# In the two FFNs of a decoder trunk: the gelu and the gate product issued behind the next weight pieces, and another order of the weight pieces in the seven-product chains

## The chip, the core and the metric

The kernel runs on one core of a Trainium2 chip. A core has a matrix engine (TensorE, PE in the profile, with its weight loads shown apart as PEld), VectorE (DVE), ScalarE (ACT), GpSimd (POOL) and SyncE (SP). Each engine works through its own list of instructions in the order in which the program issued them, and waits on semaphores for the others. The metric is the device time of one execution in microseconds; three timed executions of the kernel before stand in the table below.

## The reference

A trunk of two layers on 512 tokens of width 1024, float32. Layer 0 mixes tokens with three groups of dilated window attention, layer 1 with a gated linear recurrence. After each comes the gated ConvFFN that this change is about, between two RMS norms:

```python
def conv_ffn(x, w_up, conv_w, conv_b, w_down):
    u = causal_dwconv(x @ w_up, conv_w, conv_b)      # 3 taps along the tokens
    g, v = u[..., :D_FF], u[..., D_FF:]              # D_FF = 3072
    return (jax.nn.gelu(g, approximate=True) * v) @ w_down
```

## The kernel before

**Operands.** Each float32 matrix is split into a high and a low part (`split`, lines 152 to 154): ScalarE copies the raw tile to `hi` with rounding (L153), VectorE subtracts it from the raw tile to give `lo` (L154). Every product is three passes on TensorE, hi by hi, hi by lo and lo by hi. Raw weights come in 1 MB loads from SP (L280) into three raw buffers; their split halves go into 16 pairs of buffers (`HALVES`). A queue `pieces` holds what is to be split next, and `pump` takes pieces from its front as long as `state["live"]`, the buffers in use, allows it. `tick` is called after each step of TensorE and pumps one or two pieces. So what order the instructions of ScalarE and VectorE have is set by the order of the Python calls, nothing else reorders them.

**The up-projection of an FFN** makes 12 groups j of 256 gate features and 256 value features. A full tile is 128 features by 512 tokens, 24 matmuls (`feat`, L340). `begin` (lines 689 to 697) then computes the 3 taps: one ScalarE instruction (L679) and two on VectorE (L683) from PSUM into `u`; for a gate tile it returns the gelu (ScalarE, L695), for a value tile the product with the gate (VectorE, L697). In groups 0 to 2 and 11 `sink` calls the returned function at once, so gelu and product stand ahead of the pieces that the following `tick` splits.

**The seven-product groups.** In groups 3 to 10 the gate half is computed with seven products of quarter size instead of eight (`seven`, `chain`; matmuls at L833), the value half with full tiles, in four `quarters` each. One group is a cycle of 15 slots on TensorE: the products s1, w11, s4, w12, s2 and s3 stand at slots 0, 3, 4, 8, 9 and 14, a22 at slot 20, so in slot 5 of the next cycle; the eight other slots are quarters of value tiles. The names are those of the left operands, made of the four 512x128 blocks of one weight load: w11 and w12 are plain blocks, a22 too; s1 gets a block added by a DMA from POOL (`ahead`, L191); s2 is s1 + w11, added in place by VectorE once s1 is split (`across`, L205); s4 is w12 + s2, added in place by VectorE once w12 and w11 are split (`upper`, L209); s3 is w11 with a block added by a second DMA from POOL, issued in `upper`, once w11 is split. `stream` lists the pieces of a cycle: each has a place, and all are sorted by place. `value(0)` and `value(1)`, called v0 and v1 below, are the two value tiles of the same group, two buffers each, from the next 1 MB load. The splits of a cycle are issued about one cycle ahead of their use on TensorE.

Each chain has two PSUM banks y0 and y1. In the slot after product s4 the *seed* is issued: ScalarE saves y1 (L843) and overwrites y1 with minus y0 (L844). Product w12 adds to y0, and so waits for the seed. In the first cycle of an FFN there is no a22 of a chain before: slot 5 is empty and the seed follows one quarter later.

**The start of the seven-product part.** While the full tiles of groups 1 and 2 run, `token_sums` forms the right operands (B and T, L749 to L770) on VectorE, with splits, as a side job of the same ticks.

Of the kernel before, what the change touches and what calls it, by code (L numbers as in the profile page):

```python
# [38 lines left out]
SEVEN = range(3, 11)  # L39
# [39 lines left out]
def kernel(  # L79
# [45 lines left out]
    def psum(s="ps"):  # L125
        return pp.tile([P, 512], F32, tag="ps", name=nm(s))
# [34 lines left out]
    def parts_of(kind, raw):  # L161

        if kind == "feat":
            return [raw[:, :, m * P : (m + 1) * P] for m in range(2)]
        if kind == "value":
            return [raw[:, 2 * i : 2 * i + 2, :] for i in range(2)]
        if kind == "rows":
            return [raw[:, i : i + 1, :] for i in range(2)]
        return [raw]
# [12 lines left out]
    def blocks(i):  # L182

        raw = raws[i]
        return {
            n: raw[:, 4 * k : 4 * k + 4, m * P : m * P + P]
            for n, m, k in (("w11", 0, 0), ("w12", 0, 1), ("s1", 1, 0), ("a22", 1, 1))
        }

    def add_rows(to, src):  # L190
        nc.gpsimd.dma_start(to, src, accum_op=ALU.add)  # L191

    def ahead(i):
        assert i < state["dma"]
        add_rows(blocks(i)["s1"], plan[i][3][0][0][:, 4:8, P:256])

    def stream(i0, n):

        items = []
        for c in range(n):  # L200
            i = i0 + 2 * c

            def across(i=i):
                x = blocks(i)
                nc.vector.tensor_tensor(x["s1"], x["s1"], x["w11"], op=ALU.add)  # L205

            def upper(i=i):
                x = blocks(i)
                nc.vector.tensor_tensor(x["w12"], x["w12"], x["s1"], op=ALU.add)  # L209
                add_rows(x["w11"], plan[i][3][0][0][:, 0:4, P:256])  # L210

            def value(m, i=i + 1):
                raw = lambda: parts_of("feat", raws[i])[m]
                return (i, m), lambda: [raw()[:, :4], raw()[:, 4:]], None, m == 1

            for at, item in (
                (-6, (None, lambda i=i: ahead(i))), (0, ("s1", "s1")), (0.1, (None, across)), (1, ("w12", "w12")),
                (2, ("w11", "w11")), (2.1, (None, upper)), (4, ("s4", "w12")), (5, ("s2", "s1")), (6, value(0)),
                (8, ("a22", "a22")), (10, ("s3", "w11")), (11, value(1)),
            ):  # L220
                if c or at >= 0:
                    if isinstance(item[0], str):
                        item = ((i, item[0]), lambda i=i, h=item[1]: [blocks(i)[h]], None, item[0] == "s3")
                    items.append((CYCLE * c + at, item))
        return [item for _, item in sorted(items, key=lambda x: x[0])]
# [19 lines left out]
    def pump(limit=2):  # L245

        for _ in range(limit):
            if not pieces:
                refill()
            while pieces and pieces[0][0] is None:  # L250
                pieces.pop(0)[1]()
            if pieces and state["live"] + 2 - (pieces[0][0][1] in HALF) <= HALVES:
                key, cuts, norm, last = pieces.pop(0)
                cuts = cuts()
                his, los = [], []
                for n, raw in enumerate(cuts):
                    hi, lo = (
                        wp.tile([P] + list(raw.shape[1:]), F32R, tag=t, name=nm("w" + t)) for t in ("hi", "lo")
                    )
                    if norm is not None:  # L260
                        split_normed(hi, lo, raw, norm + n * raw.shape[1])
                    else:
                        split(hi, lo, raw)
                    his.append(hi)
                    los.append(lo)
                units[key] = (his, los)
                state["live"] += len(cuts)
                state["used"] += last
                while pieces and pieces[0][0] is None:
                    pieces.pop(0)[1]()  # L270
            while state["dma"] < len(plan) and state["dma"] - state["used"] < RAW_BUFS:
                load()
# [12 lines left out]
    def chunk():  # L285
        i = state["next"]
        state["next"] += 1
        return i

    def take(i, j):  # L290
        while (i, j) not in units:
            before = state["live"]
            pump(1)
            assert before != state["live"], (i, j, state)
        return units[i, j]

    def done(n=2):
        state["live"] -= n

    def side(steps, delay=1):  # L300
        sides.append([delay, steps])

    def tick():
        for s in list(sides):
            s[0] -= 1
            if s[0] <= 0:
                try:
                    s[0] = next(s[1])
                except StopIteration:
                    sides.remove(s)  # L310
        if not state["hold"]:
            pump(1 if state["even"] or state["live"] >= HALVES - 4 else 2)
# [201 lines left out]
    def feat_tiles(n, hT, sink, halves=False):  # L514

        if halves:
            ids = [chunk() for _ in range(n)]
            W = {}
            banks = [psum() for _ in range(2 * n)]
            for hf in range(2):  # L520
                for j in range(2 * n):
                    if not hf:
                        W[j] = take(ids[j // 2], j % 2)
                    feat(W[j], hT, banks[j], hf * 256, hf * 256 + 256)
                    if hf:
                        done()
                        sink(j, banks[j])
                    tick()
            return
        for c in range(n):  # L530
            i = chunk()
            for m in range(2):
                feat_tile(i, m, hT, lambda ps: sink(2 * c + m, ps))

    def feat_tile(i, m, hT, sink):
        ps = psum()
        feat(take(i, m), hT, ps, 0, S)
        done()
        sink(ps)
        tick()  # L540

    def rows_proj(nchunks, act, order, post, pre, eng=nc.gpsimd):

# [130 lines left out]
    def ffn(layer, hT, post, pre):  # L674
        ca, cc = ffn_cols[layer]

        def conv(ps, j):
            u = gen(s="u")
            nc.scalar.activation(  # L679
                u, ps, AF.Identity, scale=cc[:, j : j + 1], bias=cc[:, 48 + j : 49 + j]  # L680
            )
            for d, wc in ((1, ca[:, 48 + j : 49 + j]), (2, ca[:, j : j + 1])):
                nc.vector.scalar_tensor_tensor(  # L683
                    u[:, d:], ps[:, : S - d], wc, u[:, d:], op0=ALU.mult, op1=ALU.add
                )
            return u

        gv = []

        def begin(b, ps, j):  # L690
            m = b % 2
            u = conv(ps, 24 * (b // 2) + 2 * j + m)
            if b < 2:
                gv.append(u)
                return lambda: nc.scalar.activation(u, u, AF.Gelu_apprx_tanh)  # L695
            g = gv[2 * j + m]
            return lambda: nc.vector.tensor_tensor(g, g, u, op=ALU.mult)  # L697

        def sink(b, ps, j):
            begin(b, ps, j)()  # L700

        order = [([0, 1, 2, 3], range(9)), ([0], range(9, 12)), ([1], range(9, 12))]
        order += [([2, 3], [9]), ([2], [10, 11]), ([3], [10, 11])]
        prep, run = rows_proj(12, act_split(gv), order, post, pre)
        T = []
        for j in range(SEVEN[0]):
            if j == 1:
                side(token_sums(hT, T))
            if j < SEVEN[0] - 1:
                feat_tiles(2, hT, lambda b, ps: sink(b, ps, j), j == 0)  # L710
            else:
                feat_tiles(1, hT, lambda b, ps: sink(b, ps, j))
                i = chunk()
                feat_tile(i, 0, hT, lambda ps: sink(2, ps, j))
        i = seven(hT, T, begin, i)
        x_back()
        prep(3)
        for j in range(SEVEN[-1] + 1, 12):
            for b in range(j == SEVEN[-1] + 1, 4):
                if b % 2 == 0:  # L720
                    i = chunk()
                feat_tile(i, b % 2, hT, lambda ps: sink(b, ps, j))
        return run()

    kept = []
# [677 lines left out]
    hT = attention(hT, (norm_mix_post, 0), (norm_ffn_pre, 0))  # L1403
    hT = ffn(0, hT, (norm_ffn_post, 0), (norm_mix_pre, 1))
    hT = lru(hT, (norm_mix_post, 1), (norm_ffn_pre, 1))
# [29 lines left out]
```

## Time and profile before

| | |
|---|---|
| median of 3 timed executions | 1449.54 us (1449.50 to 1449.74) |
| profiled execution: its time | 1450.94 us |
| profiled execution: span from the first to the last instruction | 1449.1 us |
| mean granted TensorE clock | 0.997 |
| first FFN, seven-product part | from 563.05 us of the span on |
| second FFN, seven-product part | from 1113.03 us of the span on |

In a row of a timeline stand the start in us, the length in us, the engine, the line of the kernel, the operation, the output and inputs by name, the shape, and a count if several are merged; square brackets at the end give the idle time of the engine before it and what ended it. In a row of the table by stretches stand the stretch, its length, the busy time of each engine with its instructions, the granted clock (PEclk), the share of the DMA engines and GB/s.

### The profile page before, as it was taken

The numbers are of one execution on the slowest core, as the hardware profiler recorded it, in microseconds if no ns is written. First come the engines' busy times: TensorE is split into PE (matmuls) and PEld (weight loads), VectorE is DVE, ScalarE is ACT, GpSimd is POOL, SyncE is SP. The second block draws the span as 40 slices with busy tenths as digits, with TensorE's granted clock in tenths as the row PEclk, the third lists the DMA queues.
The fourth block names the chain that finished last, engine by engine and source line by source line (L and its number), as shares of the span: only waits on it lengthen the run. The fifth ranks groups of instructions, "written<-read, shape, count | busy, mean of one in ns | idle before, by whom it ended". The sixth has DMA issues, their size and how long they took to land.

```text
span 1449.1 us, 20565 instructions
## 1 busy us (share of the span) xinstructions
PE 1435.5 (99%) x7437; PEld 1232.3 (85%) x7437; DVE 970.6 (67%) x2115; ACT 735.1 (51%) x1644; POOL 178.3 (12%) x311
## 2 busy tenths in 40 slices
PE   9999999999999999999999999999999999999998
PEld 7888888888888898989988888888898899988886
DVE  6767747464646878877774348769778877764333
ACT  7656636262615555555543335589454655554231
POOL 0341514040402101101000001000100111000000
PEclk9999999999999999999999999999999999999999
DMA  7653536363736254554452322432434545453201
GB/s 225 208 143 114 169 118 198 115 208 106 212 100 210 90 180 89 141 132 105 140 203 87 116 74 88 131 116 73 132 126 125 137 107 140 124 190 116 87 1 59
DMA packets 142847, 189.66 MB, mean 131 GB/s; under 512 B 9313, under 2 KB 119353, under 8 KB 142233
## 3 DMA queue, kind: packets, MB, share of 16 engines
q1 hardware_dynamic: 114280, 145.48, 31.4%
q0 software_dynamic: 27616, 41.82, 12.1%
q8 instruction: 58, 0.95, 0.3%
q10 hardware_dynamic: 848, 1.05, 0.2%
q14 instruction: 45, 0.36, 0.1%
HBM read 168.83 MB, written 19.49 MB: 130 GB/s over the span
## 4 chain that ended last, share of the span: by engine, by line
PE 91%; ACT 4%; DVE 3%; issue 1%; DVEq 0%; ACTq 0%
PE ps L340 43%; PE acc L340 24%; PE ps L833 11%; PE v L1029 8%; PE v L959 1%; DVE xb L1238 1%; DVE wlo L154 1%; PE O L1180 1%; PE S L1125 1%; ACT whi L153 1%; PE S L1079 1%; ACT sig L1259 1%; PE O L340 1%; PE tr L422 1%; ACT sig L1278 0%
## 5 line engine op out<-in xcount | busy, mean ns | idle before, releaser
L340 PE MATMUL ps<-hT,whi 128*128 128x512 f32 (+1 forms) x2240 | 645.0, 373 | 0.0
L340 PEld LDWEIGHTS ps<-hT,whi 128*128 128x128 f32 x2240 | 403.9, 189 | 68.5
L340 PE MATMUL ps<-hT,wlo 128*128 128x512 f32 (+1 forms) x1120 | 415.7, 371 | 0.0
L154 DVE TENSOR_TENSOR wlo<-raw,whi 128x512 fp32r<-128x512 f32 x408 | 269.1, 688 | 186.3 <-ACT whi L153 186.3
L153 ACT ACTIVATE whi<-raw 128x512 fp32r<-128x512 f32 x408 | 244.0, 627 | 226.5 <-PE acc L340 118.2
L340 PEld LDWEIGHTS ps<-hT,wlo 128*128 128x128 f32 x1120 | 211.0, 188 | 37.1
L340 PE MATMUL acc<-whi,ahi 128*128 128x512 f32 x512 | 199.6, 390 | 0.0
L340 PE MATMUL acc<-whi,alo 128*128 128x512 f32 x512 | 199.3, 389 | 0.1
L340 PE MATMUL acc<-wlo,ahi 128*128 128x512 f32 x512 | 199.2, 389 | 0.0
L147 ACT ACTIVATE whi<-raw,first_w 128x128 fp32r<-128x128 f32 (+1 forms) x432 | 147.0, 430 | 53.2 <-PE ps L340 30.3
L683 DVE SCALAR_TENSOR_TENSOR u<-ps,cols,u 128x511 f32<-128x511 f32 x192 | 143.6, 748 | 40.9 <-ACT u L679 37.5
L148 DVE SCALAR_TENSOR_TENSOR wlo<-raw,first_w,whi 128x128 fp32r<-128x128 f32 (+1 forms) x432 | 139.7, 391 | 1.4 <-ACT whi L147 1.3
L340 PEld LDWEIGHTS acc<-whi,alo 128*128 128x128 f32 x512 | 96.1, 188 | 20.4 <-DVE alo L154 0.6
L340 PEld LDWEIGHTS acc<-whi,ahi 128*128 128x128 f32 x512 | 96.1, 188 | 19.9
L340 PEld LDWEIGHTS acc<-wlo,ahi 128*128 128x128 f32 x512 | 96.1, 188 | 19.9
L679 ACT ACTIVATE u<-ps,cols 128x512 f32<-128x512 f32 x96 | 73.8, 769 | 72.4 <-DVE ps L848 42.1
L1029 PE MATMUL v<-whi,hT 128*128 128x512 f32 x320 | 102.4, 393 | 0.0
L833 PE MATMUL ps<-T,whi 128*128 128x256 f32 x512 | 93.5, 282 | 0.0
L191 POOL DMA_DIRECT2D raw<-in_ffn_w_up_dram x32 | 41.5, 1463 | 370.0 <-DVE wlo L154 214.1
L383 POOL DMA_DIRECT2D turned<-T x36 | 19.7, 549 | 535.2 <-DVE T L377 530.3
L390 POOL DMA_DIRECT2D ft<-turned x144 | 79.1, 557 | 39.3 <-issue 20.3
L833 PEld LDWEIGHTS ps<-T,whi 128*128 128x128 f32 x512 | 80.9, 191 | 1.6
(196 smaller groups left out, 1611.0 us busy)
## 6 DMA issues: line engine op xcount, KB each, us to landing
raw<-in_ffn_w_up_dram SPq DMA_DIRECT2D x48, 1024.0 KB
raw<-in_attn_w_qkv_dram SPq DMA_DIRECT2D x67, 512.0 KB
raw<-in_ffn_w_down_dram SPq DMA_DIRECT2D x24, 1024.0 KB
raw<-in_ffn_w_up_dram POOLq DMA_DIRECT2D x32, 256.0 KB, 4.7
raw<-in_lru_w_in_dram SPq DMA_DIRECT2D x8, 1024.0 KB
turned<-T POOLq DMA_DIRECT2D x28, 256.0 KB, 2.5
ft<-turned POOLq DMA_DIRECT2D x112, 64.0 KB, 6.0
vrows<-v SPq DMA_DIRECT2D x16, 256.0 KB
```

The lines of the kernel that those rows point to most:

```text
L147: nc.scalar.activation(hi[:, k], raw[:, k], AF.Copy, scale=w)
L148: nc.vector.scalar_tensor_tensor(lo[:, k], raw[:, k], w, hi[:, k].bitcast(F32), op0=ALU.mult, op1=ALU.subtract)
L153: nc.scalar.activation(hi, raw, AF.Copy)
L154: nc.vector.tensor_tensor(lo, raw, hi.bitcast(F32), op=ALU.subtract)
L191: nc.gpsimd.dma_start(to, src, accum_op=ALU.add)
L340: mm(dst, l[a], r[b], start=start and n == 0, stop=stop and n == 2)
L383: nc.gpsimd.dma_start(d, T)
L390: nc.gpsimd.dma_start(t[32 * c : 32 * c + 32].rearrange("j (b x) -> j b x", b=4), d.rearrange("(b j) (c x) -> c j b x", j=32, c=4)[c],)
L679: nc.scalar.activation(u, ps, AF.Identity, scale=cc[:, j : j + 1], bias=cc[:, 48 + j : 49 + j])
L683: nc.vector.scalar_tensor_tensor(u[:, d:], ps[:, : S - d], wc, u[:, d:], op0=ALU.mult, op1=ALU.add)
L833: mm(y[b][:, 0:256], W[wa][0][:, k, :], right[n](ha, k), start=n in (1, 5) and k == q == 0, stop=k == 3 and q == 2, skip_group_check=True,)
L1029: mm(banks[t], hT[a][:, k, t * P : (t + 1) * P], W[b][k % 2][:, 0, :], start=(k, a, b) == (0, 0, 0), stop=(k, a, b) == (KD - 1, 1, 0),)
```

## The change

Two things. First, `feat_tile` takes what `sink` returns and calls it after `tick`; the FFN's full tiles of groups 1, 2 and 11 go through a new `tiles` whose sink is `begin` itself. So gelu and product are issued behind the pieces of that tick (and behind its side job). The other users of `feat_tile` return nothing from their sinks. Group 0 is as it was. Second, the places in `stream`: v0 goes from 6 to 3, a22 from 8 to 5, s4 from 4 to 7, s2 from 5 to 8, s3 from 10 to 11, v1 from 11 to 12. The order of a cycle's splits was s1, w12, w11, s4, s2, v0, a22, s3, v1 and is s1, w12, w11, v0, a22, s4, s2, s3, v1. `across` and `upper` keep their places. `ahead` of the next cycle, at place 9 of this one, then stands behind s2 in place of a22.

```diff
             for at, item in (
                 (-6, (None, lambda i=i: ahead(i))), (0, ("s1", "s1")), (0.1, (None, across)), (1, ("w12", "w12")),
-                (2, ("w11", "w11")), (2.1, (None, upper)), (4, ("s4", "w12")), (5, ("s2", "s1")), (6, value(0)),
-                (8, ("a22", "a22")), (10, ("s3", "w11")), (11, value(1)),
+                (2, ("w11", "w11")), (2.1, (None, upper)), (3, value(0)), (5, ("a22", "a22")), (7, ("s4", "w12")),
+                (8, ("s2", "s1")), (11, ("s3", "w11")), (12, value(1)),
             ):
...
         done()
-        sink(ps)
+        rest = sink(ps)
         tick()
+        if rest:
+            rest()
...
+        def tiles(j, i, bs):
+            for b in bs:
+                feat_tile(i, b % 2, hT, lambda ps: begin(b, ps, j))
+
...
-            if j < SEVEN[0] - 1:
-                feat_tiles(2, hT, lambda b, ps: sink(b, ps, j), j == 0)
-            else:
-                feat_tiles(1, hT, lambda b, ps: sink(b, ps, j))
-                i = chunk()
-                feat_tile(i, 0, hT, lambda ps: sink(2, ps, j))
+            if j == 0:
+                feat_tiles(2, hT, lambda b, ps: sink(b, ps, j), True)
+                continue
+            tiles(j, chunk(), (0, 1))
+            i = chunk()
+            tiles(j, i, (2, 3) if j < SEVEN[0] - 1 else (2,))
         i = seven(hT, T, begin, i)
         x_back()
         prep(3)
         for j in range(SEVEN[-1] + 1, 12):
-            for b in range(j == SEVEN[-1] + 1, 4):
-                if b % 2 == 0:
-                    i = chunk()
-                feat_tile(i, b % 2, hT, lambda ps: sink(b, ps, j))
+            tiles(j, i if j == SEVEN[-1] + 1 else chunk(), (1,) if j == SEVEN[-1] + 1 else (0, 1))
+            tiles(j, chunk(), (2, 3))
         return run()
```

## The prediction

> **What bounds the kernel now.** I read the page's busy times and chain first, then the waits of TensorE, then stretches and timelines around the waits found.
>
> ```profile
> span 1449.1 us, 20565 instructions
> PE 1435.5 (99%) x7437; PEld 1232.3 (85%) x7437; DVE 970.6 (67%) x2115; ACT 735.1 (51%) x1644; POOL 178.3 (12%) x311
> PE 91%; ACT 4%; DVE 3%; issue 1%; DVEq 0%; ACTq 0%
> ```
>
> TensorE is busy for 1435.5 of 1449.1 us. The change removes no matmul, so it can win only where TensorE waits or runs slowly. TensorE's waits by what ended them:
>
> ```profile
> PE ps L833 <- ACT ps L844: 4.6, 2, 2.3
> PE warm L1354 <- DVE one L1399: 1.5, 1, 1.5
> 575.25 0.58 PE L833 MATMUL ps<-hT,whi 128*128 128x256 f32 x2 [2.27 <-ACT ps L844]
> ```
>
> The second row is the start of the kernel. The first is the one wait of size in the body: two stalls of 2.3 us in the seven-product part, for the second instruction of the seed (L844); the third row, from TensorE's timeline, is one of them. They lie in the first cycle of each FFN. The table by stretches sets the quarter with the stall and the two products behind it against the same steps one cycle later (first FFN: rows 1 and 2 against 3 and 4; second FFN: rows 5 and 6):
>
> ```profile
> 570.07:575.25 5.18, 2.91 (x15) 2.07 (x13) 4.48 (x8) 2.88 (x7) 1.51 (x2) 1.00 0.87 237
> 575.25:579.70 4.45, 4.45 (x24) 4.45 (x25) 4.15 (x8) 2.82 (x5) 1.04 (x1) 0.62 0.69 83
> 595.02:597.77 2.75, 2.75 (x14) 2.26 (x13) 2.60 (x4) 1.41 (x4) 0.00 (x0) 1.00 1.01 123
> 597.77:600.62 2.85, 2.85 (x25) 2.84 (x24) 1.89 (x4) 2.32 (x4) 0.00 (x0) 1.00 0.00 0
> 1120.05:1125.24 5.19, 2.90 (x14) 2.07 (x12) 4.49 (x8) 2.88 (x7) 1.60 (x2) 0.98 0.82 229
> 1125.24:1129.61 4.37, 4.37 (x24) 4.37 (x25) 4.07 (x7) 2.82 (x5) 0.95 (x1) 0.63 0.76 96
> ```
>
> The waits cost 5.18 - 2.75 = 2.43 and 5.19 - 2.75 = 2.44 us. The matmuls behind them cost another 4.45 - 2.85 = 1.60 and 4.37 - 2.85 = 1.52 us: the granted clock is 0.62 and 0.63 there, where it is 1.00 one cycle later. Together 8.0 us, 0.55% of the time. That is the most that can be won here.
>
> Why is the seed late? ScalarE and VectorE around it:
>
> ```profile
> 558.02 0.63 ACT L695 ACTIVATE u<-u 128x512 f32<-128x512 f32 x1 [4.87 <-DVE u L683]
> 561.16 0.76 ACT L679 ACTIVATE u<-ps,cols 128x512 f32<-128x512 f32 x1
> 563.85 0.64 ACT L695 ACTIVATE u<-u 128x512 f32<-128x512 f32 x1 [1.92 <-DVE u L683]
> 564.38 0.61 ACT L153 ACTIVATE whi<-raw 128x512 fp32r<-128x512 f32 x1
> 564.90 0.77 ACT L679 ACTIVATE u<-ps,cols 128x512 f32<-128x512 f32 x1
> 565.57 2.18 ACT L153 ACTIVATE whi<-raw 128x512 fp32r<-128x512 f32 x4
> 567.91 0.62 ACT L153 ACTIVATE whi<-raw 128x512 fp32r<-128x512 f32 x1
> 572.34 2.19 ACT L153 ACTIVATE whi<-raw 128x512 fp32r<-128x512 f32 x4 [3.80 <-DVE raw L209]
> 574.43 0.36 ACT L843 ACTIVATE part<-ps 128x256 f32<-128x256 f32 x1
> 574.82 0.37 ACT L844 ACTIVATE ps<-ps 128x256 f32<-128x256 f32 x1
> ```
>
> ```profile
> 556.40 1.53 DVE L683 SCALAR_TENSOR_TENSOR u<-ps,cols,u 128x511 f32<-128x511 f32 x2
> 559.21 1.29 DVE L154 TENSOR_TENSOR T<-B,T 128x512 fp32r<-128x512 f32 x2 [1.28 <-ACT T L153]
> 562.23 1.52 DVE L683 SCALAR_TENSOR_TENSOR u<-ps,cols,u 128x511 f32<-128x511 f32 x2
> 565.03 0.69 DVE L154 TENSOR_TENSOR wlo<-raw,whi 128x512 fp32r<-128x512 f32 x1 [1.28 <-ACT whi L153]
> 565.70 1.53 DVE L683 SCALAR_TENSOR_TENSOR u<-ps,cols,u 128x511 f32<-128x511 f32 x2
> 567.27 0.69 DVE L697 TENSOR_TENSOR u<-u,u 128x512 f32<-128x512 f32 x1
> 571.62 0.69 DVE L209 TENSOR_TENSOR raw<-raw 128x512 f32<-128x512 f32 x1
> 565.70:572.30 6.60, 6.60 (x42) 5.95 (x41) 6.50 (x11) 2.83 (x6) 0.31 (x1) 1.00 0.76 249
> ```
>
> ScalarE is not short of time: it idles 3.80 us, because the split of s4 waits for `upper` (L209) on VectorE. Behind that stand s2 and the two buffers of v0 (the four splits at 572.34), then the seed. VectorE is the late one: from 565.70 to 572.30 it works 6.50 of 6.60 us. And it had idled 1.28 us twice just before (559.21, 565.03), waiting for splits that ScalarE held behind a gelu (L695), which itself waited 4.87 and 1.92 us for VectorE's taps. The two engines wait for one another in turn.
>
> **The change part by part.** Nothing is added or removed; instructions and their durations stay, so every term is a wait.
>
> *New order of pieces.* In the first cycle the pieces ahead of the seed become v0 (two splits), a22, s4; s2 comes behind it. One split after L209 remains in place of four. Splits in a row are (2.19 - 0.62) / 3 = 0.52 us apart, so with nothing else changed L844 ends at 575.19 - 3 x 0.52 = 573.62. TensorE reaches product w12 at 570.07 + 2.75 = 572.82 and started 0.06 us after L844 before: it would wait to 573.68, 0.86 us in place of 2.43. v0 and a22 use the 3.80 us in which ScalarE idled. They need v0's load, issued here:
>
> ```profile
> 565.75 0.37 SPq L280 DMA_DIRECT2D raw<-in_ffn_w_up_dram  x1
> ```
>
> 1.05 MB at the 237 GB/s of the first stretch above are 4.4 us, so I estimate landing at 566.12 + 4.4 = 570.5. Three splits to 572.1, s4 to 572.6, seed to 573.4: still no longer a wait than 0.86 us.
>
> *Gelu and product behind the pieces.* Two effects, worked out on the rows above. VectorE: the taps of the last full tile stood behind the `lo` of 565.03, which waited for ScalarE. That split now precedes the gelu, so the tile bounds the taps. How soon ScalarE can read a tile shows an earlier one, with the last matmul of the last tile below it:
>
> ```profile
> 551.94 0.39 PE L340 MATMUL ps<-hT,wlo 128*128 128x512 f32 x1
> 552.37 0.78 ACT L679 ACTIVATE u<-ps,cols 128x512 f32<-128x512 f32 x1 [1.94 <-PE ps L340]
> 562.82 0.39 PE L340 MATMUL ps<-hT,wlo 128*128 128x512 f32 x1
> ```
>
> It began 0.04 us after the last matmul ended (551.94 + 0.39 = 552.33). So here it can at 562.82 + 0.39 + 0.04 = 563.25, takes 0.77 us, and VectorE starts at 564.05, 1.65 us before 565.70. What follows to L209 is the same 6.6 us of work (the product moves within it), so `upper` ends at 570.65, not 572.30. The load: it is freed by the `lo` of s3, split at 564.38. In the new order the gelu of 558.02 ends at about 559.2 (the product ahead of the taps at 556.40 adds 0.6), taps and two splits follow to 561.0, VectorE's taps and two `lo` to 563.0: the load goes out some 2.7 us earlier and lands by 567.8. Then v0 and a22 are split by 569.4, s4 from 570.7 to 571.2, and the seed (0.39 from L843 to L844, and 0.37) ends at 572.0, 0.8 us before TensorE needs it at 572.82. So the wait goes, and the low clock behind it.
>
> What is late next? With TensorE 4.0 us earlier, VectorE's debt counts more: in this cycle y0's sum (L848) must be done before product s3. Behind L209 stand eleven subtractions, sums and products, one pair of taps and L848 itself: at 1.29 - 0.69 = 0.60 us each and 1.55 for the taps, 570.65 + 12 x 0.60 + 1.55 = 579.4. Product s3 starts two products and four quarters after 572.82, at 572.82 + 2.85 + 2 x 2.75 = 581.2. So 1.8 us remain; that cover gone, TensorE would wait here in place of the seed, twice in all.
>
> *Later cycles* (seven in each FFN). Here the seed waits for nothing but TensorE:
>
> ```profile
> 614.72 0.38 ACT L843 ACTIVATE part<-ps 128x256 f32<-128x256 f32 x1 [0.93 <-PE ps L833]
> 615.13 0.37 ACT L844 ACTIVATE ps<-ps 128x256 f32<-128x256 f32 x1
> 618.71 0.40 PE L833 MATMUL ps<-hT,whi 128*128 128x256 f32 x2
> 611.83 0.63 ACT L153 ACTIVATE whi<-raw 128x512 fp32r<-128x512 f32 x1 [1.94 <-PE ps L340]
> 601.76 0.37 SPq L280 DMA_DIRECT2D raw<-in_ffn_w_up_dram  x1
> 611.81:632.74 20.93, 20.93 (x134) 18.98 (x134) 16.14 (x26) 11.48 (x20) 2.59 (x3) 1.00 0.51 126
> ```
>
> L844 ends at 615.50 and TensorE comes at 618.71: 3.2 us in hand. In the new order the buffers run full as now (the split at 611.83 waits 1.94 us for TensorE), and by my count of the live buffers the split of a22, just ahead of the seed, gets the buffer of product s4, which the seed awaits too. So the seed moves back by one split, 0.52 us, and 2.7 us stay: cost nothing. Without that cover it would be the delay plus a slow clock, 14 times. v0 is split two slots earlier, 2.8 us; its load, issued at 601.76, lands by my 4.4 us at 606.5, 6 us before. VectorE has 16.14 us of work in 20.93, so the debt is paid within a cycle. TensorE uses a22 at slot 20 and s4, s2 in the next cycle: a place later or earlier in a list that runs one cycle ahead costs nothing.
>
> *The move of `ahead`*: POOL's DMA waits for its load alone and keeps its rank between the two `upper` DMAs of POOL, so nothing moves. SP's loads keep their rank too: v0's goes out with the `lo` of s3, the next chain's with that of v1. *Group 11*: gelus and products go behind pieces too; TensorE waits for nothing there. Zero.
>
> **Sum.** 2.43 + 2.44 + 1.60 + 1.52 = 8.0 us. The profiled execution took 1450.94 us with a span of 1449.10; it would be 1442.9. Its time is 1.4 us over the median of the timed runs, and from that median I get 1449.54 - 8.0 = 1441.5 us.
>
> [...]
>
> **The rivals.**
>
> *Shortened, not gone.* VectorE doesn't gain its 1.65 us, because ScalarE is held by something else. Then 0.86 us stay at each place: 1441.5 + 1.7 = 1443.2 without the slow clock, 1446.3 with all of it. No row shows a wait of that size, so I keep both ends. For it: VectorE works without a gap. Against: its two gaps end in ScalarE's splits behind a gelu.
>
> *The wait moves to the load: no change.* Should v0's load land late, v0 holds ScalarE, in-order, as s4 did. To give 575.19 again, four splits and the seed must start at 572.34, so the load must land 1.8 us after my estimate of its unmoved time. Against: the 237 GB/s.
>
> *The slow clock stays.* The two slow stretches are not the waits' doing, and come at that place of the program anyway: 1449.54 - 4.87 = 1444.7 us. Against: one cycle later, and in all other rows here, the same steps run at 1.00. [...]
>
> *Slower.* In 14 later cycles the seed stands behind v0 and a22. If these hold it over 2.7 us, TensorE waits each time, and the clock falls: at 0.5 us over, 14 x (0.5 + 1.56) = 29 us, 1470 us; at 0.1 us and full clock 1443. It decides beyond 2.7 us. For: the buffers are full and a22 lives longer in one. Against: 6 us at the load, and a22's buffer is freed by the product the seed awaits anyway.
>
> **Chances.** Both waits and the slow clock gone 0.71; shortened 0.13; slow clock stays 0.02; no change 0.06; slower 0.08. The range: 1440.8 (a little under the full 8.0 us) to 1446.4, the upper end of "shortened"; outside lie no change, slower, and little else. A measurement of this kernel tells 0.2%, 2.9 us, from no change: below 1446.6 is faster, which holds the first three cases: 0.86; same 0.06; slower 0.08.
>
> **What would show it.** In the page after: the row of TensorE's waits for the seed gone or far below 2.3 us; the clock 1.00 in the first cycle of both FFNs; the first cycle to the second some 4.0 us shorter; `upper` ending about 1.6 us earlier against TensorE's first product; no wait of 1.28 us on VectorE behind a gelu; later cycles still 20.93 us. Wrong if TensorE shows waits for L844 in many cycles, or for a split, a load or L848 in the first.

## The result, and the profile after

The changed kernel takes 1443.04 us (1442.91 to 1443.06), the kernel before, run beside it, 1449.5 us (1448.13 to 1449.74). The ratio is 0.9957, with a 95% interval of 0.9942 to 0.9971: 6.5 us faster. The forecast was 1441.5 us. One execution among the experiments, of the run with K = 6 in the later cycles, took 1784.23 us at a mean granted clock of 0.752 and is left out of its comparison. The profiled execution after took 1443.05 us, against 1450.94 before, which is 7.9 us less. Why these two differences are not the same is the first question below.

The page after, its span and busy times:

```profile
span 1441.3 us, 20577 instructions
PE 1432.1 (99%) x7437; PEld 1229.6 (85%) x7437; DVE 968.8 (67%) x2115; ACT 735.6 (51%) x1644; POOL 177.7 (12%) x311
```

TensorE's waits after, by what ended them (total, times, longest):

```profile
PE warm L1358 <- DVE one L1403: 1.5, 1, 1.5
PE v L963 <- ACT whi L147: 0.6, 2, 0.3
PE v L963 <- ACT hT L442: 0.2, 1, 0.2
```

The row of the seed, 4.6 us in 2 waits, is gone, and nothing has taken its place: what is left are the start of the kernel and waits of 0.3 us and less. TensorE's busy time fell too, from 1435.5 to 1432.1 us with the same 7437 matmuls. That is mostly the clock, 0.62 and 0.63 behind the waits before and 1.00 now, as the table by stretches shows (stretch, its length, busy time of each engine with its instructions, then granted clock, DMA share, GB/s). The rows are the quarter that held the wait and the two products behind it, in the first FFN and in the second. The lines of the code have moved by 2 to 4: L848, L837 and L852 here are L844, L833 and L848 of before.

```profile
570.25:572.99 2.74, 2.74 (x14) 2.26 (x13) 2.74 (x5) 2.15 (x5) 1.44 (x2) 1.00 0.61 174
572.99:575.85 2.86, 2.86 (x26) 2.85 (x25) 2.83 (x6) 2.00 (x4) 1.12 (x1) 1.00 0.92 114
1116.18:1118.93 2.75, 2.75 (x14) 2.27 (x13) 2.75 (x5) 2.15 (x5) 1.46 (x2) 1.00 0.53 160
1118.93:1121.78 2.85, 2.85 (x25) 2.84 (x24) 2.81 (x6) 1.61 (x4) 1.09 (x1) 1.00 0.98 120
```

These four stretches took 5.18, 4.45, 5.19 and 4.37 us before, 19.19 together; now they take 11.20. That is 7.99 us, all that was there. The start of the kernel came 0.18 us later in this execution (the first product of the part at 563.23, before at 563.05), and 7.99 - 0.18 = 7.8 us is the whole difference of the spans, 1449.1 to 1441.3. The two long stretches behind them agree: from the products of the first FFN's row to the second FFN's seven-product part 533.33 us before and 533.31 after, from the last of the four stretches to the end 319.5 both times. So nothing was won or lost anywhere else.

How the seed came early shows in the timelines. ScalarE in the first cycle:

```profile
563.43 0.78 ACT L681 ACTIVATE u<-ps,cols 128x512 f32<-128x512 f32 x1 [1.27 <-PE ps L340]
564.10 2.18 ACT L153 ACTIVATE whi<-raw 128x512 fp32r<-128x512 f32 x4
567.74 1.78 ACT L153 ACTIVATE whi<-raw 128x512 fp32r<-128x512 f32 x3 [0.66 <-DMA raw<-in_ffn_w_up_dram]
570.81 0.63 ACT L153 ACTIVATE whi<-raw 128x512 fp32r<-128x512 f32 x1 [1.29 <-DVE raw L209]
571.35 0.36 ACT L847 ACTIVATE part<-ps 128x256 f32<-128x256 f32 x1
571.74 0.37 ACT L848 ACTIVATE ps<-ps 128x256 f32<-128x256 f32 x1
```

VectorE at the same place:

```profile
564.24 1.53 DVE L685 SCALAR_TENSOR_TENSOR u<-ps,cols,u 128x511 f32<-128x511 f32 x2 [1.61 <-ACT u L681]
570.03 0.69 DVE L209 TENSOR_TENSOR raw<-raw 128x512 f32<-128x512 f32 x1
578.70 0.42 DVE L852 TENSOR_TENSOR ps<-part,ps 128x256 f32<-128x256 f32 x1
```

And TensorE, at products w12 and s3:

```profile
572.99 0.40 PE L837 MATMUL ps<-hT,whi 128*128 128x256 f32 x2
581.32 0.40 PE L837 MATMUL ps<-T,whi 128*128 128x256 f32 x2
```

VectorE's last taps now wait for the tile itself (1.61 us, ended by ScalarE's L681), no longer for a split behind a gelu. `upper` (L209) starts at 570.03 where it started at 571.62. Of ScalarE's splits only one is left behind it (570.81), the others are done during what was the idle time of 3.80 us. The seed ends at 571.74 + 0.37 = 572.11, 0.88 us before TensorE's product w12 (572.99), which starts without a wait.

**Two differences, 7.9 and 6.5 us.** The timed executions of before lie on three levels. Beside each stands the span and the mean granted clock of the same execution:

```
time, us             span, us           granted clock
1448.01 to 1448.13   1446.2 to 1446.3   0.999
1449.29 to 1449.77   1447.5 to 1448.0   0.998
1450.98 to 1451.40   1449.2 to 1449.6   0.997
```

The steps are 1.5 us, about what one of the two slow stretches costs. In the clock records of before's trace each lasts 3.41 us at half clock. The first starts at 575.52 us of the span, 0.27 behind the end of the wait, the second at 1125.07, 0.17 before its wait ends (so the prediction's row at 1120.05 has a clock of 0.98). The table by stretches of before, cut there (3.41 us ahead of each slow stretch, then the slow stretch; first FFN, second FFN):

```profile
572.11:575.52 3.41, 1.14 (x6) 0.65 (x5) 2.69 (x5) 3.15 (x7) 1.67 (x2) 1.00 0.92 216
575.52:578.93 3.41, 3.41 (x18) 3.41 (x18) 3.13 (x5) 2.55 (x5) 0.78 (x1) 0.50 0.76 91
1121.66:1125.07 3.41, 1.29 (x6) 0.75 (x4) 2.71 (x6) 2.71 (x6) 1.43 (x2) 1.00 0.80 234
1125.07:1128.48 3.41, 3.24 (x15) 3.24 (x16) 3.11 (x6) 2.84 (x6) 1.12 (x1) 0.50 0.94 119
```

I read the levels as executions of before with none, one or two slow stretches. The profile (1450.94 us) has both, the median of 1449.5 has one. After has no wait and one level. The numbers close to 0.2 us: 1443.04 + 4.87 for the two waits gives 1447.9, where the lowest level is 1448.05; with one slow stretch more, at 1.5, the difference is 6.4, where 6.5 was measured; the four stretches of 19.19 us together make 8.0, against the 7.9 of the profiles.

### The profile page after: what moved, and what is told of

It is laid out like the page before. It is cut to its first block, busy times and chain, and to the rows that moved or that the text cites. A ratio compares the mean times of both kernels' runs of the same rounds, so it can differ in the third digit from the quotient of the medians.

```text
span 1441.3 us, 20577 instructions
## 1 busy us (share of the span) xinstructions
PE 1432.1 (99%) x7437; PEld 1229.6 (85%) x7437; DVE 968.8 (67%) x2115; ACT 735.6 (51%) x1644; POOL 177.7 (12%) x311
## 4 chain that ended last, share of the span: by engine, by line
PE 92%; ACT 4%; DVE 3%; issue 1%; DVEq 0%; ACTq 0%
PE ps L340 44%; PE acc L340 24%; PE ps L837 11%; PE v L1033 8%; PE v L963 1%; DVE xb L1242 1%; PE O L1184 1%; PE S L1129 1%; PE S L1083 1%; DVE wlo L154 1%; ACT sig L1263 1%; ACT whi L153 1%; PE O L340 1%; PE tr L422 1%; ACT sig L1282 0%
## 5 line engine op out<-in xcount | busy, mean ns | idle before, releaser
L681 ACT ACTIVATE u<-ps,cols 128x512 f32<-128x512 f32 x96 | 74.0, 770 | 82.3 <-DVE ps L852 41.8
L837 PE MATMUL ps<-T,whi 128*128 128x256 f32 x512 | 92.8, 280 | 0.0
L837 PEld LDWEIGHTS ps<-T,whi 128*128 128x128 f32 x512 | 80.1, 189 | 1.6
```

What stands on the lines that cost most here:

```text
L681: nc.scalar.activation(u, ps, AF.Identity, scale=cc[:, j : j + 1], bias=cc[:, 48 + j : 49 + j])
L837: mm(y[b][:, 0:256], W[wa][0][:, k, :], right[n](ha, k), start=n in (1, 5) and k == q == 0, stop=k == 3 and q == 2, skip_group_check=True,)
```

## The experiments

The theory: in the first cycle TensorE waited for the seed because ScalarE and VectorE held one another up, and each of the two edits takes part of that wait; the slow clock follows from the wait. The rivals: one edit does it all; the wait moves elsewhere; the slow clock belongs to the place and not to the wait; the margin of the later cycles is not what the prediction took it for. The ratios below compare the mean with that of the kernel before, run beside each experiment.

**The order of the pieces alone** (gelu and product where they were):

```diff
-                (2, ("w11", "w11")), (2.1, (None, upper)), (4, ("s4", "w12")), (5, ("s2", "s1")), (6, value(0)),
-                (8, ("a22", "a22")), (10, ("s3", "w11")), (11, value(1)),
+                (2, ("w11", "w11")), (2.1, (None, upper)), (3, value(0)), (5, ("a22", "a22")), (7, ("s4", "w12")),
+                (8, ("s2", "s1")), (11, ("s3", "w11")), (12, value(1)),
```

> The new order of pieces, with gelu and product ahead of them as before. My theory, that each half of the change shortens the wait and only both end it: upper still ends near 572.3 us, one split and the seed follow, TensorE waits about 0.86 us for L844 in the first cycle of each FFN: 1443.0 + 1.7 = 1444.8 us if so short a wait leaves the clock alone, up to 1447.9 with two slow stretches of 1.56 us. Rival, the order alone ends the wait: 1443.0 us, no wait for L844. Rival, the order is not what counts: 1449.5 us with waits of 2.3 us.

Measured: 1445.12 us (1444.99 to 1445.39), ratio 0.9966 (0.9953 to 0.9978). The row of TensorE's waits:

```profile
PE ps L833 <- ACT ps L844: 1.7, 2, 0.9
```

Its timelines of ScalarE, VectorE and TensorE, put together by time:

```profile
571.08 2.20 ACT L153 ACTIVATE whi<-raw 128x512 fp32r<-128x512 f32 x4 [2.45 <-DMA raw<-in_ffn_w_up_dram]
571.72 0.68 DVE L209 TENSOR_TENSOR raw<-raw 128x512 f32<-128x512 f32 x1
573.58 0.37 ACT L844 ACTIVATE ps<-ps 128x256 f32<-128x256 f32 x1
574.00 0.39 PE L833 MATMUL ps<-hT,whi 128*128 128x256 f32 x1 [0.85 <-ACT ps L844]
```

The wait of 0.85 us is the 0.86 forecast, but by the other path: ScalarE waits 2.45 us for v0's load, and that load, no longer `upper`, holds the four splits. With v0 ahead and its load not earlier, the load is what is late. The two paths lie close together: the fourth split could start at about 571.08 + 3 x 0.52 = 572.6, and `upper` ended at 572.40. So the agreement with 0.86 is in part luck.

**Gelu and product behind the pieces alone** (the changed kernel with the old list of places):

> Gelu and product behind the pieces, the order of pieces as before. My theory: upper ends 1.6 us earlier against TensorE, near 570.7 us, but four splits still stand between it and the seed (4 x 0.52 us), so L844 ends near 573.5 and TensorE, there at 572.8 to 573.0, waits 0.6 to 0.8 us in each FFN: 1444.4 to 1444.6 us with the full clock, up to 1447.7 with two slow stretches. Rival, the gelu's place alone ends the wait: 1443.0 us. Rival, VectorE gains nothing from it: 1449.5 us, upper at 572.3 us.

Measured: 1444.56 us (1444.38 to 1444.63), ratio 0.9961 (0.9949 to 0.9974). Its row of TensorE's waits:

```profile
PE ps L837 <- ACT ps L848: 1.0, 2, 0.5
```

Its timelines, in the same way:

```profile
569.97 0.69 DVE L209 TENSOR_TENSOR raw<-raw 128x512 f32<-128x512 f32 x1
570.69 2.20 ACT L153 ACTIVATE whi<-raw 128x512 fp32r<-128x512 f32 x4 [3.66 <-DVE raw L209]
573.19 0.37 ACT L848 ACTIVATE ps<-ps 128x256 f32<-128x256 f32 x1
573.61 0.51 PE L837 MATMUL ps<-hT,whi 128*128 128x256 f32 x2 [0.51 <-ACT ps L848]
```

`upper` ends at 570.66, as with both edits: this edit alone brings its 1.65 us. ScalarE still idles 3.66 us and has four splits behind `upper`, so 0.51 us stay. Each edit alone leaves a wait, and only both leave none. Neither kernel has a slow stretch (granted clock 0.999 in all five executions of each).

**The wait put back, at chosen lengths.** The changed kernel, with the first of the seed's two instructions issued several times over in the first cycle of each FFN (it writes the same values again; these kernels are two lines longer, so their L850 is the changed kernel's L848):

```diff
                     def seed():
+                        for _ in range(K if j == SEVEN[0] else 0):
+                            nc.scalar.activation(z, c, AF.Copy)
                         nc.scalar.activation(z, c, AF.Copy)
                         nc.scalar.activation(c, a, AF.Copy, scale=-1.0)
```

With K = 4:

> The changed kernel with the first instruction of the seed given five times in place of once in the first cycle of each FFN (same result): 4 x 0.39 = 1.56 us of ScalarE ahead of L844. In the trace after, L848 ends 0.88 us before TensorE's product w12. My theory: a wait of 1.56 - 0.88 + 0.06 = 0.74 us in each FFN, 1443.0 + 1.5 = 1444.5 us with the full clock, 1447.6 if a wait of 0.7 us is also followed by a slow stretch of 1.56 us. Rival, the margin is larger or something else is awaited: 1443.0 us.

Measured: 1444.79 us (1444.72 to 1445.09), ratio 0.9963 (0.995 to 0.9977), with two waits of 0.7 us and no slow stretch (granted clock 0.999 in the profiled execution). So the margin in the first cycle is real: of 4 x 0.40 us of delay, 0.88 were absorbed and 0.7 waited for.

With K = 6:

> The changed kernel, first instruction of the seed seven times in the first cycle of each FFN: a wait of 6 x 0.39 - 0.88 + 0.06 = 1.52 us, costing about 1.75 us each with the 0.25 us by which the earlier short waits cost more than their length: 1443.0 + 3.5 = 1446.5 us with no slow stretch. The timed executions of the kernel before fell into three levels with granted clocks of 0.999, 0.998 and 0.997 and spans 1.5 us apart, which I read as none, one or two slow stretches. [...]

Measured: 1446.56 us (1446.41 to 1446.66), ratio 0.998 (0.9971 to 0.9989): two waits of 1.5 us, one level of time, and no slow stretch (granted clock 0.999 in the profiled execution).

With K = 8, the length of before's waits:

> As the run with six more, with eight more: a wait of 8 x 0.39 - 0.82 = 2.30 us, the length in the kernel before, of another origin. Cost 2.5 us each: 1448.1 us with no slow stretch, 1449.6 with one, 1451.1 with two. [...] Rival, the slow stretch in the kernel before came from something else than the wait: all at 1448.1.

Measured: 1451.01 us (1448.23 to 1451.57), ratio 1.0001 (0.9992 to 1.001): the kernel before again. Its executions fall on the same three levels: 2 near 1448.2, 3 near 1449.7, 6 from 1451.0 to 1451.6. The profiled one has its two waits alike in TensorE's waits:

```profile
PE ps L837 <- ACT ps L850: 4.7, 2, 2.3
```

The table by stretches (the quarter with the wait, then the two products; first FFN, second FFN) does not have what follows them alike:

```profile
570.22:575.47 5.25, 2.91 (x15) 2.08 (x13) 2.88 (x5) 4.40 (x12) 2.56 (x2) 1.00 0.75 145
575.47:579.91 4.44, 4.44 (x24) 4.44 (x25) 3.89 (x7) 2.82 (x5) 0.00 (x0) 0.62 0.35 44
1120.27:1125.52 5.25, 2.91 (x15) 2.07 (x13) 2.88 (x5) 4.41 (x12) 2.55 (x2) 1.00 0.71 140
1125.52:1128.47 2.95, 2.95 (x24) 2.95 (x25) 2.44 (x4) 2.71 (x5) 0.00 (x0) 1.00 0.57 70
```

The same wait, 5.25 us of quarter both times, is followed once by 4.44 us at clock 0.62 and once by 2.95 at 1.00. So in this run the slow stretch did not always follow the wait. It is worth 4.44 - 2.95 = 1.49 us, the step between the levels.

The same table, cut as that of before: 3.41 us ahead of the slow stretch, then the slow stretch, and for the second FFN the same cuts 549.55 us later, the distance between the two slow stretches in before's trace:

```profile
572.04:575.45 3.41, 1.09 (x5) 0.56 (x3) 1.06 (x2) 3.15 (x10) 1.27 (x1) 1.00 0.78 96
575.45:578.87 3.42, 3.40 (x16) 3.40 (x17) 2.85 (x5) 2.84 (x5) 0.00 (x0) 0.50 0.46 58
1121.59:1125.00 3.41, 1.58 (x7) 0.97 (x6) 1.56 (x3) 3.16 (x9) 1.71 (x2) 1.00 0.63 80
1125.00:1128.41 3.41, 2.90 (x24) 2.90 (x25) 2.38 (x4) 3.19 (x7) 0.00 (x0) 1.00 0.62 77
```

The first wait lies almost whole in the first row, with 3.41 - 1.09 = 2.32 us of idle TensorE, and the next row is at half clock. The second is cut by the edge between the rows into 1.83 and 0.51 us, and the clock stays full. In before's rows 2.27 and 2.12 us of idle TensorE stand ahead of the slow stretches. That the place of the wait against such an edge decides is my reading of these four waits; no run here moved the place alone.

With K = 12:

> As before with twelve more: a wait of 12 x 0.39 - 0.82 = 3.86 us, longer than the slow stretch of 3.4 us seen. Cost 4.1 us each: 1451.2 us with no slow stretch, 1454.3 with two. [...]

Measured: 1455.3 us (1455.23 to 1456.75), ratio 1.0039 (1.0026 to 1.0053), about 1 us over the 1454.3 expected with two slow stretches. The two waits are 4.0 us each, and the table by stretches has slow products behind both (first FFN, second FFN):

```profile
576.93:581.16 4.23, 4.23 (x24) 4.23 (x25) 3.68 (x6) 2.71 (x5) 0.00 (x0) 0.66 0.00 0
1128.65:1133.94 5.29, 5.29 (x25) 5.29 (x26) 4.75 (x8) 2.82 (x5) 0.00 (x0) 0.50 0.00 0
```

In the second row all is at half clock. By its clock of 0.66 the first row holds 0.34 x 4.23 / 0.5 = 2.9 us at half clock. In the second place the 3.41 us in which the wait ends, and the next, are both at half clock:

```profile
1127.82:1131.23 3.41, 2.58 (x12) 2.59 (x13) 2.07 (x4) 2.99 (x6) 0.00 (x0) 0.50 0.09 11
1131.23:1134.64 3.41, 3.41 (x16) 3.31 (x16) 3.38 (x6) 0.63 (x1) 0.00 (x0) 0.50 0.12 26
```

That is 6.82 us in a row, twice the length of before's slow stretches. The first of the two rows, already at half clock, held 0.83 us of the wait, and the next one was at half clock too. The other executions were not profiled; their granted clock was 0.996 or 0.995, lower than the 0.997 of every execution of the kernel before on its highest level, which I read as more than two stretches of 3.41 us in each.

**The margin of the later cycles.** The same repetition for the seven later cycles of each FFN (`j > SEVEN[0]`). First K = 6, which delays the seed by 2.34 us, under the 2.81 us in hand:

> The changed kernel with six more in the 14 later cycles: 2.34 us against 2.81 in hand. Theory: no wait for the seed, 1443.0 us, within 0.3. Rival, the delay is paid elsewhere (taps and sums behind it on ScalarE): over 1444 us without a wait for the seed.

Measured: 1443.48 us (1443.18 to 1443.69 in the four executions compared), ratio 0.9955 (0.9942 to 0.9969). TensorE's waits have no row for the seed. The time is 0.4 us above the changed kernel, a little over the 0.3 expected. The cycles do not hold it: from the first product of the part to product s3 of its last cycle this trace takes 164.63 us in the first FFN and 164.63 in the second, the changed kernel's 164.62 both times. The 0.4 us lie between the two parts, where the edit does nothing (381.71 us in place of 381.32); why is open.

Then K = 9, 0.8 us past the margin:

> The changed kernel with the first instruction of the seed given ten times in place of once in the 14 later cycles: 9 x 0.39 = 3.51 us ahead of L848, against 2.81 us in hand in the trace after (L848 ends at 612.05, product w12 starts at 614.86). My theory: a wait of 0.76 us in each of 14 cycles, 10.6 us, 1453.7 us with the full clock; with a slow stretch of 1.56 us behind each, 1475.5 us. Rival, ScalarE catches up elsewhere and the cover is larger: 1443.0 us. Rival, the delay carries on to the taps and the sums behind it: above 1480 us.

Measured: 1458.94 us (1458.69 to 1459.1), ratio 1.0061 (1.0048 to 1.0073). The row of TensorE's waits:

```profile
PE ps L837 <- ACT ps L850: 11.7, 14, 0.8
```

The table by stretches, a quarter of a later cycle and the two products behind:

```profile
591.10:594.84 3.74, 2.91 (x14) 2.07 (x12) 0.30 (x1) 3.49 (x10) 0.35 (x1) 1.00 1.10 137
594.84:597.79 2.95, 2.95 (x24) 2.95 (x25) 2.40 (x4) 1.81 (x4) 0.00 (x0) 1.00 0.00 0
```

The margin is where it was forecast: 14 waits, 0.83 us each. No slow clock shows behind them (1.00 in these rows, 0.999 granted in all five executions). Yet the time rose by 15.9 us, not 11.7. A wait cost more than its row: the quarter takes 3.74 in place of 2.75 us, 0.99, and the two products 2.95 in place of 2.85, 0.10. That is 1.09 us each, 15.3 for 14; the other 0.6 us are outside these rows. The expectation of 1453.7 us at full clock was low by 5.2 us, mostly because it charged each wait with its length alone. The short waits of the first cycle show the same: two of 0.51 us cost 1444.56 - 1443.04 = 1.5 us, two of 0.85 cost 2.1, so each cost 0.2 to 0.25 more than it lasted.

## Why the prediction was right, and the term that was mis-sized

*The bound, and where the time was.* Right. All of the difference lies in the four stretches that the prediction quoted, 7.99 us against its 8.0.

*VectorE 1.65 us earlier.* Right: L209 ends at 570.72 in place of 572.31, 1.6 us. The taps start at 564.24 where the working gave 564.05, and 0.18 of the 0.19 is the later start of the kernel.

*v0's load.* Right. Forecast to go out at 563.0 and land by 567.8; ScalarE's split got it at 567.74. The row of its issue:

```profile
562.66 0.37 SPq L280 DMA_DIRECT2D raw<-in_ffn_w_up_dram  x1
```

ScalarE waited 0.66 us for it, but then 1.29 us more for `upper` (the row at 570.81), so the load could have come 1.29 us later without moving the seed. That this load could become the late one was a rival; the run with the order alone shows it happening, at a wait of 0.85 us and not the 2.4 of the rival, and the second edit is what takes it away by freeing the buffer earlier (the load goes out at 562.66, with the order alone at 565.92).

*Order alone: 0.86 us left.* The size was right (0.85), the reason only partly: the prediction bounded it by the splits behind `upper`, and held the load to be early enough (570.5); it came at 571.08 and bound.

*The seed 0.8 us before TensorE.* It is 0.88. *What is late next:* y0's sum ends at 578.70 + 0.42 = 579.12 (forecast 579.4), 2.2 us before product s3 at 581.32 (forecast 1.8 us).

*Later cycles.* Right. The timelines of ScalarE and TensorE in the second cycle:

```profile
611.69 0.37 ACT L848 ACTIVATE ps<-ps 128x256 f32<-128x256 f32 x1
614.86 0.40 PE L837 MATMUL ps<-hT,whi 128*128 128x256 f32 x2
```

The table by stretches, from that cycle to the next:

```profile
609.99:630.92 20.93, 20.93 (x135) 18.98 (x134) 16.15 (x26) 11.47 (x20) 2.59 (x3) 1.00 0.51 126
```

614.86 - 612.06 = 2.8 us in hand, forecast 2.7; the cycle is still 20.93 us. The rival "slower" has its place and its threshold right: at 2.34 us of delay nothing waits, at 3.5 us all 14 do. Its price was too high: it put 0.5 + 1.56 us to each short wait, where one of 0.83 us cost 1.1, at full clock.

*The slow clock, 3.1 us.* This is the term that was mis-sized. Against its own execution the sum was right: 1450.94 - 8.0 = 1442.9, and the profile after has 1443.05. The prediction then took the same 8.0 from the median, 1449.54. But the 1.4 us between that execution and the median, which the prediction saw and named, were one slow stretch: the profile had two, the median had one by its level and its clock of 0.998, so that only 1.5 of the 3.1 us was there to win. 1449.54 - 4.87 - 1.5 = 1443.2, against the measured 1443.04. The sign that could have been read: the page's time lay 1.4 us above the median, and above all three timed runs, about the size of one of its own terms.

*Slow clock stays at its place.* Excluded by the run with waits of 1.5 us and by the changed kernel: same place, clock 1.00.

## What to carry to other kernels

Where two in-order engines wait for one another in turn, look at what stands in each queue ahead of the instruction that the other awaits: here a gelu ahead of a split on one engine, and taps behind that split's `lo` on the other, put `upper` back by 1.6 us, and three splits between `upper` and the seed that could stand elsewhere did the rest of a wait that cost 2.4 us, with ScalarE busy half the time. Before a term is taken from the median, ask whether the median has it: if the profiled execution lies off the median by the size of one of the terms, subtract from the profiled time, or count that term by how often it occurs. An edit that uses a margin (here 0.4 of 3.2 us, in 14 cycles) should have that margin worked out from the two rows that set it, since past it every cycle pays.

## What the runs showed of the hardware

- The slow stretches behind TensorE's waits, by the length of the wait. Waits of up to 0.9 us: none, in 100 waits. 1.5 us: none, in 20. 2.3 us: in 38 of 68 waits of the kernel before, and in 15 of 22 put back by hand, 53 of 90 together. 4.0 us: after all 10, and of double length (6.82 us at half clock) at least once. For the waits that were not profiled these counts are read from the levels of time and clock.
- In before's trace each slow stretch lasted 3.41 us at a granted clock of 0.50, with 2.27 and 2.12 us of idle TensorE in the 3.41 us ahead of it. In the run with K = 8 2.32 us stood ahead of the slow stretch; at the other place 1.83 us stood ahead of 3.41 us at clock 1.00. In the run with K = 12 3.41 us at half clock, with 0.83 us of idle time, were followed by 3.41 us more at half clock. What decides whether a wait of 2.3 us is followed by a slow stretch is not shown.
- A short wait of TensorE (0.51, 0.83 and 0.85 us) cost 0.2 to 0.25 us more than the wait that the trace lists; at 0.83 us 0.1 of it lay in the two products behind, at clock 1.00. Why is not settled.
